# Two PSUM banks instead of four for the large products beside stick-breaking attention

## The chip, the cores and the metric

The kernel runs on one core of one Trainium2 chip. The metric is device time in microseconds (us), the median of several runs. In the text PE is TensorE's matmul pipe, DVE is VectorE, ACT is ScalarE, POOL is GpSimd and SP is SyncE, which here only issues DMAs. PSUM, where TensorE writes its results, has eight banks of 128x512 fp32 values; a tile here takes a whole bank.

## What is computed

A trunk of two layers on 512 tokens of width 1024. The first layer mixes tokens with a gated short convolution, the second with stick-breaking attention; both also attend to 256 memory tokens, and both end in a SwiGLU block. The change touches the second layer only, in these lines of the reference:

```python
kv = (rmsnorm(x, kv_norm) @ w_kv_shared).reshape(b, s_len, 2, SB_HEADS, HEAD_DIM)   # 12 heads of 64
k_sh, v_sh = kv[:, :, 0], kv[:, :, 1]
...
z = jnp.einsum("bhtd,bhsd->bhts", qb, kb) * scale          # 4 blocks of 128 queries
log_not = jnp.where(causal, jax.nn.log_sigmoid(-z), 0.0)
tail = lax.cumsum(log_not, axis=3, reverse=True) - log_not
a = jnp.where(causal, jnp.exp(jax.nn.log_sigmoid(z) + tail), 0.0)
outs.append(jnp.einsum("bhts,bhsd->bhtd", a, vb))
...
x = x + jnp.concatenate([y_main, y_mem], axis=-1) @ w_o[i]
x = x + swiglu(rmsnorm(x, ffn_norm[i]), w_gate[i], w_up[i], w_down[i])
```

## The kernel before

Every fp32 operand is split in two parts (`wh`, `wl` and the like: high part by an ACT copy, low part by a DVE subtraction), and each product is made of three matmuls: high x high, high x low, low x high (`three`, L345). So TensorE does three passes over all weights, and weights are split on the fly: they arrive by DMA in two `raw` buffers and are split into nine `w` buffers (L35, L36, L169), which are taken in turn and come free when the last matmul that reads them is done.

PSUM is shared by two groups of four banks. `acc` (L129) serves the large products: queries `q`, values `v`, keys `k`, the output projection `o` and its late part `ol`. `att` (L132) serves everything of attention: scores `z`, transposes `at`, the weighted sums `av`, and the gate and up products of the SwiGLU block. A tile takes its group's next bank in turn, and its first matmul waits until the tile that held the bank before has been read for the last time.

The order of work around the change is one program, in which the large products are the main work and stick-breaking is a generator (`stick`, L904) whose steps are slipped in between. After each few matmuls of the main work `lanes.pump` runs the steps that are due by a count of matmul columns (`STICK_PACE`). There are 48 steps: six pairs of heads, two heads in each, four blocks of queries. A step issues the scores `z` of its block (two matmuls), two sigmoids on ACT (`sn`, `sp`), two causal masks on POOL, a reversed running product on DVE (the scan of `sn`) and a multiplication (`sp`). Two steps later the weights are transposed on PE (`at`) and split (`aTh` on ACT, `aTl` on DVE). Five steps later, for every second block, the weighted sum `av` is taken (`weighted`, L939). When a head is done its sum is copied and added (`pv_s` on ACT, `ysf` on DVE), and when a pair is done the result is split into `ys` (ACT, then DVE).

The main work beside it is, in order: for three blocks of 256 columns, the values (`values`, L883: `by_token`, four token tiles) and the keys (two tiles); then the output projection `out_proj_late` (L665), for two halves of the columns, with the memory heads (`ym`) and the first four pairs `ys0` to `ys3` as its left side; then the last two pairs (`ol`), the norms, and the SwiGLU block (its first products are `gu`). `by_token` (L396) takes four banks, one a token tile. It runs a piece of the weights over all four tiles, then the next piece, so every bank is in use until the last piece. When the output projection asks for `ys` of a pair that is not yet issued, `ys_late` (L996) issues stick-breaking steps until it is (`lanes.until`).

After this a scheduler orders the instructions of each engine; on each engine they then run strictly in that order.

Of the kernel before, what the change touches and what calls it, by code (L numbers as in the profile page):

```python
# [9 lines left out]
F32 = mybir.dt.float32  # L10
# [6 lines left out]
P = 128  # L17
# [89 lines left out]
def trunk(ctx: ExitStack, tc: tile.TileContext, x, mem, mix_norm, a_in, conv_w, b_in,  # L107
# [13 lines left out]
    ps = ctx.enter_context(tc.tile_pool(name="ps", bufs=4, space=bass.MemoryType.PSUM))  # L121

    def slot(shape, dtype, name):
        return apool.tile(shape, dtype, tag="a", name=name)

    def t2(shape, dtype, name):
        return tpool.tile(shape, dtype, tag="t2", name=name)

    def acc(name):  # L129
        return ps.tile([P, 512], F32, tag="acc", name=name, bufs=4)  # L130

    def att(name):  # L132
        return ps.tile([P, 512], F32, tag="att", name=name, bufs=4)
# [211 lines left out]
    def three(dst, a, b, first, last):  # L345

        mm(dst, a(HI), b(HI), first, False)
        mm(dst, a(HI), b(LO), False, False)
        mm(dst, a(LO), b(HI), False, last)
# [46 lines left out]
    def by_token(w, pieces, c0, n, lhs, ntok, name, done, tail=1):  # L396


        banks = [acc(f"{name}{t}") for t in range(ntok)]
        got = []  # L400
        nk = sum(len(p) for p in pieces)
        at = 0
        for i, (kts, wp) in enumerate(rows(w, pieces, c0, n)):
            got.append((at, kts, wp))
            at += len(kts)
            if i >= len(pieces) - tail and i != len(pieces) - 1:
                continue
            for t in range(ntok):
                for a, ks, (wh, wl) in got:
                    for j, k in enumerate(ks):  # L410
                        three(banks[t][:, :n], lambda hl: lhs(k, hl, t), lambda hl: (wh, wl)[hl][:, j, :],
                              a + j == 0, a + j == nk - 1)
                        lanes.pump()
                if i == len(pieces) - 1:
                    done(t, banks[t])
            got = []
# [39 lines left out]
    banks = first.run(hmix, nx.chains, as_they_come)  # L456
# [6 lines left out]
    def queries(b, name):  # L463


        q = slot([P, 2, S], F32R, name)
        for hh in range(2):
            r = hh * HD
            own, other = slice(r, r + HD), slice(HD - r, P - r)
            nc.scalar.activation(q[own, hh, :], b[own, :], AF.Copy, scale=SCALE)  # L470
            nc.vector.scalar_tensor_tensor(q[other, hh, :], b[own, :], SCALE, q[own, hh, :].bitcast(F32),
                                           ALU.mult, ALU.subtract)
        return q
# [128 lines left out]
    for cc in range(3):  # L602
        cg, cus = [], []
        for c in range(2):
            f = 2 * cc + c
# [7 lines left out]
            t = t2([P, S], F32, f"cgs{f}")  # L613
            nc.scalar.activation(t, b, AF.Copy)
            cg.append(t)
        for c, get in enumerate(cols(a_in[0], 2 * MAIN + cc * 256)):
            f = 2 * cc + c
# [10 lines left out]
        for c, get in enumerate(cols(a_in[0], cc * 256)):  # L628
            f = 2 * cc + c
# [13 lines left out]
    def residual(t, hf, b, ss, name):  # L643
        part = xt[t][:, hf * 512:(hf + 1) * 512]
        nc.vector.tensor_tensor(part, b, part, ALU.add)
        if ss is not None:
            square_sum(ss[t], xt[t], hf, f"{name}{t}")
# [4 lines left out]
    def ylhs(ys):  # L652
        return lambda k, hl, t: ys(k)[:, hl, t * P:(t + 1) * P]
# [11 lines left out]
    def out_proj_late(layer, ys, last, opening, then):  # L665

        for hf in range(2):
            by_token(w_o[layer], [[6, 7], [0, 1], [2, 3]], hf * 512, 512, ylhs(ys), NT,
                     f"o{layer}{hf}", lambda t, b: residual(t, hf, b, None, f"oa{layer}"))
        wp = [list(rows(w_o[layer], [[4, 5]], hf * 512, 512))[0][1] for hf in range(2)]  # L670
        last()
        opening.prepare()
        ss = sums(f"sso{layer}")
        for t in range(NT):
            for hf in range(2):
                b = acc(f"ol{layer}{t}{hf}")
                for j, k in enumerate((4, 5)):
                    three(b, lambda hl: ylhs(ys)(k, hl, t), lambda hl: wp[hf][hl][:, j, :], j == 0, j == 1)
                    lanes.pump()
                residual(t, hf, b, ss, f"ob{layer}")  # L680
            then(t, rstd_of(ss[t], f"o{layer}{t}"))
# [222 lines left out]
    def stick(pace):  # L904
        weight, aT, pvs, yfs = {}, {}, {}, {}

        def weigh(p, hh, i):

            q, (kd, kl) = qs[p], ks[p]
            n, nm = (i + 1) * P, f"{p}{hh}{i}"  # L910
            z = att(f"z{nm}")[:, :n]
            scores_of(z, q, hh, i, kd[:, hh, :n], kl[:, hh, :n])
            sn = t2([P, S], F32, f"sn{nm}")
            sp = t2([P, S], F32, f"sp{nm}")
            nc.scalar.activation(sn[:, :n], z, AF.Sigmoid, scale=-1.0)
            causal(sn[:, i * P:n], 1.0)
            nc.scalar.activation(sp[:, :n], z, AF.Sigmoid)
            causal(sp[:, i * P:n], 0.0)
            back = sn[:, 1:n][:, ::-1]
            nc.vector.tensor_tensor_scan(back, back, back, 1.0, ALU.mult, ALU.bypass)  # L920
            nc.vector.tensor_tensor(sp[:, :n - 1], sp[:, :n - 1], sn[:, 1:n], ALU.mult)
            weight[p, hh, i] = sp
            if (p, hh, i) == (PAIRS - 1, 1, NT - 1):
                load_table(AF.Silu, sp[:, n - 1:n])

        def turn(p, hh, i):
            n, u, nm = (i + 1) * P, i % 2, f"{p}{hh}{i}"
            if u == 0:
                aT[p, hh, i // 2] = [slot([P, 4, 256], F32R, f"aT{hl}{nm}") for hl in "hl"]
            sp = weight.pop((p, hh, i))  # L930
            b = att(f"at{nm}")
            for j in range(i + 1):
                transpose(b[:, j * P:(j + 1) * P], sp[:, j * P:(j + 1) * P], ident)
            src = b[:, :n].rearrange("p (j c) -> p j c", j=i + 1)
            dst = [a[:, 0:i + 1, u * P:(u + 1) * P] for a in aT[p, hh, i // 2]]
            hi_of(dst[HI], src)
            lo_of(dst[LO], src, dst[HI])

        def weighted(p, hh, ip):  # L939
            head, r = 2 * p + hh, hh * HD  # L940
            if ip == 0:
                pvs[head] = att(f"av{head}")
                if hh == 0:
                    yfs[p] = t2([P, S], F32, f"ysf{p}")
            pv, a = pvs[head], aT.pop((p, hh, ip))
            top = 2 * ip + 1
            for part, j in [(HI, 0)] + [(LO, j) for j in range(top + 1)] + [(HI, j) for j in range(1, top + 1)]:
                s0 = P if j == top else 0
                mm(pv[0:P if part == HI else HD, ip * 256 + s0:(ip + 1) * 256], value(j, head, part == HI),
                   a[part][:, j, s0:256], part == HI and j == 0, part == HI and j == top)  # L950
            if ip == 1:
                stacked_pv(pvs.pop(head), r, yfs[p], f"s{head}")
                if hh == 1:
                    ymain[p] = split_y(yfs.pop(p), f"ys{p}")

        steps = [(p, hh, i) for p in range(PAIRS) for hh in range(2) for i in range(NT)]
        N = len(steps)
        for n in range(N + SUM_AFTER):
            if n < N:
                while ks[steps[n][0]] is None:  # L960
                    yield 1000
                weigh(*steps[n])
            if 0 <= n - TURN_AFTER < N:
                turn(*steps[n - TURN_AFTER])
            if 0 <= n - SUM_AFTER < N and steps[n - SUM_AFTER][2] % 2:
                p, hh, i = steps[n - SUM_AFTER]
                weighted(p, hh, i // 2)
            yield int(pace * (steps[min(n, N - 1)][2] + 1) / 2.5)

    banks = first.run(hq, nq.chains)  # L970
# [5 lines left out]
    for c2 in range(1, 3):  # L976
        for c, get in enumerate(cols(b_in[0], c2 * 256)):
            b = acc(f"q{c2}{c}")
            by_feature(b, get(), hq, 0, S)
            qs[2 * c2 + c] = queries(b, f"q{2 * c2 + c}")  # L980
    for c2 in range(3):
        values(c2)
        if c2 == 0:
            lanes.finish(mat)
        for c, get in enumerate(cols(w_kv_shared, c2 * 256)):
            b = acc(f"k{c2}{c}")
            by_feature(b, get(), hkv, 0, S)
            p = 2 * c2 + c
            kd = slot([P, 2, S], F32R, f"kd{p}")
            kl = key_lo[p % len(key_lo)]  # L990
            keys(b, kd, kl)
            ks[p] = kd, kl
            if p == 1:
                sticks = lanes.spawn(stick(STICK_PACE))
# [56 lines left out]
```

## Time and profile before

| | |
|---|---|
| median of 3 runs | 1145.6 us (1145.08 to 1145.99) |
| the profiled execution | 1145.12 us |
| its span, first to last instruction | 1143.4 us |
| PE busy, share of the span | 1130.9 us, 99% |
| DVE busy | 699.5 us, 61% |
| ACT busy | 524.1 us, 46% |
| mean granted TensorE clock | 0.998 |

The profile lists for each engine how long it was busy, what ended its idle time, and when each instruction started. Matmuls are pipelined, so their listed durations overlap: how much time one costs is read from the distance between the starts of consecutive ones. The names are those of the tiles, with their numbers left out: `o` is any tile of the output projection.

### The profile page before, as it was taken

To read this page: it belongs to the slowest core of one execution; us is meant where nothing else is said; L and a number is where in the kernel's file an instruction comes from. 1 tells how busy PE (TensorE), PEld (TensorE's weight loads), DVE (VectorE), ACT (ScalarE), POOL (GpSimd) and SP (SyncE) were. 2 spreads that over 40 slices of the span, in tenths; PEclk is the share of its full clock that TensorE was granted. 3 is DMA by queue.
4 is the path that set the end of the run, shared out by engine and by line. 5 is a ranking of instruction groups with operands and counts; after the bars stand their busy time and mean duration, and the time that the engine had idled before them with its cause. 6 is when DMAs were issued, how large, how long until landed. Compare 5 with 4: busy or idle time off the path is not lost.

```text
span 1143.4 us, 14862 instructions
## 1 busy us (share of the span) xinstructions
PE 1130.9 (99%) x5844; PEld 963.2 (84%) x5844; DVE 699.5 (61%) x1044; ACT 524.1 (46%) x896; POOL 76.3 (7%) x155
## 2 busy tenths in 40 slices
PE   9999999999999999999999999999999999999997
PEld 9898888988888888888988988788888888888886
DVE  5767453553774468434678799986546844485335
ACT  7555423533432344233666677665434332353223
POOL 1100000000000001000100123321000000000000
PEclk9999999999999999999999999999999999999999
DMA  8332422247332742414222211122274244542311
GB/s 259 111 111 74 144 78 74 74 142 190 111 111 74 219 108 79 141 62 130 75 74 75 74 56 56 38 75 92 74 220 123 66 143 149 109 148 76 126 57 74
DMA packets 97456, 122.10 MB, mean 107 GB/s; under 512 B 2217, under 2 KB 73963, under 8 KB 97387
## 3 DMA queue, kind: packets, MB, share of 16 engines
q1 hardware_dynamic: 93040, 112.73, 30.1%
q0 software_dynamic: 4224, 8.39, 4.3%
q8 instruction: 46, 0.75, 0.3%
q14 instruction: 23, 0.19, 0.1%
q10 hardware_dynamic: 123, 0.03, 0.0%
HBM read 119.05 MB, written 2.10 MB: 106 GB/s over the span
## 4 chain that ended last, share of the span: by engine, by line
PE 92%; issue 3%; DVE 2%; ACT 1%; POOL 1%; DMA 1%; POOLq 0%; ACTq 0%; SPq 0%; DVEq 0%
PE u L136 22%; PE g L136 19%; PE A_d L136 6%; PE d L136 5%; PE o L136 5%; PE N_d L136 4%; PE S_d L136 4%; PE gu L136 4%; PE bg L136 3%; PE v L136 3%; PE k L136 2%; PE pa L136 2%; PE cg L136 2%; PE q L136 1%; PE pb L136 1%
## 5 line engine op out<-in xcount | busy, mean ns | idle before, releaser
L157 DVE TENSOR_TENSOR wl<-raw,wh 128x1024 fp32r<-128x1024 f32 x180 | 220.0, 1222 | 281.3 <-PE u L136 136.5
L154 ACT ACTIVATE wh<-raw 128x1024 fp32r<-128x1024 f32 x180 | 191.0, 1061 | 264.6 <-PE u L136 75.8
L819 ACT ACTIVATE sg<-g 128x512 f32<-128x512 f32 x40 | 23.9, 598 | 105.5 <-PE g L136 105.5
L136 PE MATMUL g<-hffn0h,wh 128*128 128x512 f32 x160 | 62.3, 389 | 0.0
L136 PE MATMUL g<-hffn0l,wh 128*128 128x512 f32 x160 | 62.3, 389 | 0.0
L136 PE MATMUL g<-hffn1h,wh 128*128 128x512 f32 x160 | 62.3, 389 | 0.0
L136 PE MATMUL g<-hffn1l,wh 128*128 128x512 f32 x160 | 62.3, 389 | 0.0
L136 PE MATMUL g<-hffn0h,wl 128*128 128x512 f32 x160 | 62.2, 389 | 0.0
L136 PE MATMUL u<-hffn0h,wh 128*128 128x512 f32 x160 | 62.2, 389 | 0.0
L136 PE MATMUL u<-hffn0l,wh 128*128 128x512 f32 x160 | 62.2, 389 | 0.0
L136 PE MATMUL u<-hffn0h,wl 128*128 128x512 f32 x160 | 62.2, 389 | 0.0
L136 PE MATMUL g<-hffn1h,wl 128*128 128x512 f32 x160 | 62.2, 389 | 0.0
L136 PE MATMUL u<-hffn1h,wh 128*128 128x512 f32 x160 | 62.2, 389 | 0.0
L136 PE MATMUL u<-hffn1l,wh 128*128 128x512 f32 x160 | 62.2, 389 | 0.0
L136 PE MATMUL u<-hffn1h,wl 128*128 128x512 f32 x160 | 62.2, 389 | 0.0
L136 PE MATMUL d<-wh,hid 128*128 128x512 f32 x192 | 59.7, 389 | 0.0
L154 ACT ACTIVATE wh<-b_d 128x1024 fp32r<-128x1024 f32 x32 | 33.7, 1060 | 34.2 <-PE u L136 15.3
L920 DVE TENSOR_TENSOR_SCAN sn<-sn 128x127 f32<-128x127 f32 (+3 forms) x48 | 40.3, 840 | 4.8 <-POOL sn L901 4.4
L136 PEld LDWEIGHTS d<-wh,hid 128*128 128x128 f32 x192 | 36.0, 188 | 7.5
L157 DVE TENSOR_TENSOR wl<-b_d,wh 128x1024 fp32r<-128x1024 f32 x32 | 38.9, 1221 | 4.1 <-PE N_d L136 2.3
L136 PE MATMUL d<-wl,hid 128*128 128x512 f32 x96 | 37.4, 389 | 0.0
L136 PEld LDWEIGHTS u<-hffn0l,wh 128*128 128x128 f32 x160 | 30.0, 188 | 6.3
(777 smaller groups left out, 2937.9 us busy)
## 6 DMA issues: line engine op xcount, KB each, us to landing
raw<-in_w_gate_dram SPq DMA_DIRECT2D x22, 1024.0 KB, 5.3
raw<-in_w_up_dram SPq DMA_DIRECT2D x22, 1024.0 KB, 5.4
raw<-in_w_down_dram SPq DMA_DIRECT2D x12, 1024.0 KB, 6.6
raw<-in_a_in_dram SPq DMA_DIRECT2D x8, 1024.0 KB, 5.5
b_d<-in_w_down_dram SPq DMA_DIRECT2D x8, 1024.0 KB, 7.5
raw<-in_w_o_dram SPq DMA_DIRECT2D x12, 512.0 KB, 3.6
raw<-in_w_kv_shared_dram SPq DMA_DIRECT2D x6, 1024.0 KB, 5.0
raw<-in_w_mem_kv_dram SPq DMA_DIRECT2D x4, 1024.0 KB, 5.2
```

Of the source, the lines that this page charges most:

```text
L136: nc.tensor.matmul(dst, a, b, start=start, stop=stop)
L154: keep(nc.scalar.activation(dst, src, AF.Copy))
L157: keep(nc.vector.tensor_tensor(dst, src, hi.bitcast(F32), ALU.subtract))
L819: nc.scalar.activation(sg, bg, AF.Silu)
L920: nc.vector.tensor_tensor_scan(back, back, back, 1.0, ALU.mult, ALU.bypass)
```

## The change

`acc` now takes its banks from two groups of two (`acc` and `mid`) in turn, which makes four as before, except while a flag `few` is set. The flag is set after the queries' products, before the first values, and cleared in `out_proj_late` before the late part. While it is set, `acc` has two banks, and the weighted sums `av` take the two banks of `mid`; the four banks of `att` are then left to `z` and `at`. `by_token` no longer takes its four banks at the start: while the flag is set it waits for all pieces of the weights and then runs all of them for one token tile after the other, and each tile takes its bank when its turn comes.

```diff
+    few, turns = [False], [0]
+
     def acc(name):
-        return ps.tile([P, 512], F32, tag="acc", name=name, bufs=4)
+        turns[0] += 1
+        return ps.tile([P, 512], F32, tag="acc", name=name, bufs=2) if few[0] or turns[0] % 2 else mid(name)
+
+    def mid(name):
+        return ps.tile([P, 512], F32, tag="mid", name=name, bufs=2)
...
     def by_token(w, pieces, c0, n, lhs, ntok, name, done, tail=1):
-        banks = [acc(f"{name}{t}") for t in range(ntok)]
+        if few[0]:
+            tail = len(pieces)
+        banks = [acc(f"{name}{t}") for t in range(ntok) if tail < len(pieces)]
...
             for t in range(ntok):
+                if t == len(banks):
+                    banks.append(acc(f"{name}{t}"))
...
         last()
+        few[0] = False
         opening.prepare()
...
             if ip == 0:
-                pvs[head] = att(f"av{head}")
+                pvs[head] = mid(f"av{head}")
...
+    few[0] = True
     for c2 in range(3):
         values(c2)
```

How it moves instructions is seen at three places. In the names, the first number of `z412`, `at410`, `sp403` is the pair, the second the head in the pair, the third the block; `o101` is layer 1, first half of the columns, token tile 1; what follows a `_` is a running number.

On PE, where the output projection first reads `ys3`, the rows before are:

```order
L136 MATMUL o101_6471<-wh197_6672,ys2_6432 128x512
L136 MATMUL o101_6471<-wl197_6673,ys2_6432 128x512
L136 MATMUL o101_6471<-wh197_6672,ys2_6432 128x512
L136 MATMUL z412_6741<-kd4_6322,q4_5066 128x384
L136 MATMUL z412_6741<-kl0_4548,q4_5066 128x384
L143 MATMUL at410_6756<-ident_77,sp410_6683 128x128
L136 MATMUL av8_6760<-aTh400_6623,v20_6077 128x256
L136 MATMUL av8_6760<-aTl400_6624,v20_6077 64x256
L136 MATMUL av8_6760<-aTl400_6624,v20_6077 64x128
L136 MATMUL o100_6470<-wh197_6672,ys3_6711 128x512
L136 MATMUL o100_6470<-wl197_6673,ys3_6711 128x512
L136 MATMUL av8_6760<-aTh400_6623,v20_6077 128x128
```

and with the change they are:

```order
L143 MATMUL o101_6724<-wl194_6474,ym10_5099 128x512
L150 MATMUL at410_6713<-ident_77,sp410_6644 128x128
L143 MATMUL o101_6724<-wh194_6473,ym10_5099 128x512
L143 MATMUL o101_6724<-wh194_6473,ym11_5284 128x512
L143 MATMUL o101_6724<-wl194_6474,ym11_5284 128x512
L143 MATMUL o101_6724<-wh194_6473,ym11_5284 128x512
L143 MATMUL z413_6731<-kd4_6322,q4_5066 128x512
L143 MATMUL z413_6731<-kl0_4548,q4_5066 128x512
L143 MATMUL o100_6487<-wh197_6483,ys3_6672 128x512
L143 MATMUL o100_6487<-wl197_6484,ys3_6672 128x512
L150 MATMUL at411_6744<-ident_77,sp411_6682 128x128 x2
L143 MATMUL o101_6724<-wh195_6477,ys0_5848 128x512
```

Before, 54 matmuls of `o` stand ahead of the first that reads `ys3`: all that the first two pieces of the weights give to four token tiles, and a few of the third. Now 21 do: 15 of token tile 0, which are all that it has without `ys3`, and 6 of tile 1.

On PE, at the transposes of the last step, the rows before are:

```order
L136 MATMUL o113_6805<-wh202_7061,ys2_6432 128x512
L136 MATMUL o113_6805<-wl202_7062,ys2_6432 128x512
L136 MATMUL o113_6805<-wh202_7061,ys2_6432 128x512
L143 MATMUL at513_7108<-ident_77,sp513_7040 128x128 x4
L136 MATMUL o113_6805<-wh202_7061,ys3_6711 128x512
L136 MATMUL o113_6805<-wl202_7062,ys3_6711 128x512
L136 MATMUL o113_6805<-wh202_7061,ys3_6711 128x512
L136 MATMUL av11_7131<-aTh510_7015,v20_6077 128x256
```

and with the change they are:

```order
L143 MATMUL o111_7052<-wh200_6983,ys0_5848 128x512
L143 MATMUL o111_7052<-wl200_6984,ys0_5848 128x512
L143 MATMUL o111_7052<-wh200_6983,ys0_5848 128x512
L150 MATMUL at513_7062<-ident_77,sp513_7001 128x128 x4
L143 MATMUL o111_7052<-wh200_6983,ys1_6162 128x512
L143 MATMUL o111_7052<-wl200_6984,ys1_6162 128x512
L143 MATMUL o111_7052<-wh200_6983,ys1_6162 128x512
L143 MATMUL o111_7052<-wh202_6989,ys2_6432 128x512
```

Before, three matmuls of `o` were left when the last transposes came. Now 45 are left: nine of tile 1 of the second half, all 18 of tile 2 and all 18 of tile 3.

On DVE, where the order calls the scan of `sn` `SCALAR_TENSOR_TENSOR`, the second half's first weight pieces (`wl200`, `wl202`) are split at other places. Before, the rows around the first of them are:

```order
L157 TENSOR_TENSOR aTl310_6501<-at311_6531,aTh310_6500 128x2x128
L921 TENSOR_TENSOR sp313_6522<-sp313_6522,sn313_6521 128x511
L157 TENSOR_TENSOR wl200_6932<-raw198_6806,wh200_6931 128x1024
L920 SCALAR_TENSOR_TENSOR sn400_6558<-sn400_6558 128x127
L921 TENSOR_TENSOR sp400_6559<-sp400_6559,sn400_6558 128x127
L157 TENSOR_TENSOR aTl312_6569<-at312_6570,aTh312_6568 128x3x128
```

and with the change:

```order
L933 TENSOR_TENSOR sp503_6858<-sp503_6858,sn503_6857 128x511
L656 TENSOR_TENSOR x2_75<-o102_6814,x2_75 128x512
L164 TENSOR_TENSOR wl200_6984<-raw198_6976,wh200_6983 128x1024
L932 SCALAR_TENSOR_TENSOR sn510_6889<-sn510_6889 128x127
L933 TENSOR_TENSOR sp510_6890<-sp510_6890,sn510_6889 128x127
L164 TENSOR_TENSOR aTl502_6900<-at502_6901,aTh502_6899 128x3x128
```

It stood ahead of step 400, and now it stands ahead of step 510, behind the residual sum of tile 2; `wl202` moved likewise from ahead of step 410 to behind the scan of step 511.

## Rows read from the trace of the kernel before

**Rows 1.** The page: busy times, and the granted clock in 40 slices.

```profile
PE 1130.9 (99%) x5844; PEld 963.2 (84%) x5844; DVE 699.5 (61%) x1044; ACT 524.1 (46%) x896; POOL 76.3 (7%) x155
...
PEclk9999999999999999999999999999999999999999
```

**Rows 2.** Stretches: length, busy us of each engine, granted clock, DMA.

```profile
640.00:660.00 20.00, 20.00 (x152) 19.01 (x152) 18.17 (x31) 14.70 (x36) 6.07 (x17) 1.00 0.23 74
...
712.00:736.00 24.00, 22.75 (x124) 17.71 (x121) 21.84 (x38) 17.17 (x39) 9.39 (x20) 1.00 0.13 44
736.00:767.00 31.00, 30.11 (x163) 25.20 (x164) 28.61 (x48) 18.08 (x40) 9.83 (x20) 1.00 0.23 69
```

**Rows 3.** Waits of PE, 640 to 784 us: total, times, longest.

```profile
PE z L136 <- DVE aTl L157: 1.1, 2, 0.7
PE o L136 <- DVE kl L157: 0.6, 1, 0.6
PE ol L136 <- ACT ys L154: 0.4, 1, 0.4
```

**Rows 4.** PE in order of time: start, us, instruction, [idle before <- releaser].

```profile
735.92 0.50 PE L136 MATMUL o<-wh,ys 128*128 128x512 f32 x1
...
765.97 0.39 PE L136 MATMUL o<-wl,ys 128*128 128x512 f32 x1
766.19 0.63 PE L136 MATMUL o<-wh,ys 128*128 128x512 f32 x2
766.66 0.39 PE L136 MATMUL o<-wl,ys 128*128 128x512 f32 x1
...
783.72 0.39 PE L136 MATMUL gu<-hffn1h,wh 128*128 128x256 f32 x1
```

**Rows 5.** DVE in order of time, around the split of `ys3`.

```profile
721.40 0.68 DVE L921 TENSOR_TENSOR sp<-sp,sn 128x511 f32<-128x511 f32 x1
722.00 1.22 DVE L157 TENSOR_TENSOR wl<-raw,wh 128x1024 fp32r<-128x1024 f32 x1
723.40 0.48 DVE L920 TENSOR_TENSOR_SCAN sn<-sn 128x127 f32<-128x127 f32 x1 [0.19 <-POOL sn L901]
...
729.68 1.22 DVE L920 TENSOR_TENSOR_SCAN sn<-sn 128x511 f32<-128x511 f32 x1 [0.96 <-POOL sn L901]
...
733.13 0.48 DVE L920 TENSOR_TENSOR_SCAN sn<-sn 128x127 f32<-128x127 f32 x1 [0.19 <-POOL sn L901]
...
736.42 0.73 DVE L157 TENSOR_TENSOR ys<-ysf,ys 128x512 fp32r<-128x512 f32 x1
737.07 0.50 DVE L921 TENSOR_TENSOR sp<-sp,sn 128x255 f32<-128x255 f32 x1
```

**Rows 6.** PE in order of time, at values and the first keys.

```profile
621.72 0.28 PE L136 MATMUL v<-wh,hkvh 128*128 128x256 f32 x1
621.84 0.28 PE L136 MATMUL v<-wl,hkvh 128*128 128x256 f32 x1
...
643.50 0.28 PE L136 MATMUL v<-wh,hkvh 128*128 128x256 f32 x1
...
674.08 0.28 PE L136 MATMUL v<-wh,hkvh 128*128 128x256 f32 x1
...
681.61 0.36 PE L136 MATMUL v<-wh,hkvh 128*128 128x256 f32 x1
```

**Rows 7.** DVE in order of time, at the reads of values and keys.

```profile
621.53 0.68 DVE L521 TENSOR_TENSOR ymf<-pv,pv 64x512 f32<-64x512 f32 x1 [1.08 <-ACT pv L520]
...
624.24 0.41 DVE L157 TENSOR_TENSOR v<-v,v 128x256 fp32r<-128x256 f32 x1
...
643.77 0.69 DVE L157 TENSOR_TENSOR kl<-k,kd 64x512 fp32r<-64x512 f32 x1 [1.08 <-ACT kd L154]
...
680.70 0.69 DVE L157 TENSOR_TENSOR kl<-k,kd 64x512 fp32r<-64x512 f32 x1 [0.34 <-ACT kd L154]
```

**Rows 8.** The page: DMA issues, KB each, median us from issue to landing.

```profile
raw<-in_w_o_dram SPq DMA_DIRECT2D x12, 512.0 KB, 3.6
```

## The prediction, made before the changed kernel ran

> **What bounds the kernel now.** I read the page first: PE is busy for 99% of the span, and its clock is granted in full in all 40 slices [rows 1]. Nearly every microsecond in which PE waits is then a microsecond of the result, and little is to be won: PE's total work does not change, and the change can only add or take away waits. The stretches come next [rows 2]. In the span as a whole DVE is 61% busy, but while stick-breaking runs it is a second bound: 18.2 of 20 us from 640 to 660 and 50.5 of 55 us from 712 to 767. An order of work that needs DVE's results sooner than before finds no spare DVE time. Third, PE's waits in the affected stretch [rows 3]: 1.1 us of `z` for the DVE read that frees an `att` bank (twice), 0.6 us of `o` for the read of a key tile, 0.4 us of `ol` for `ys`. That is the change's target: four banks for `z` and `at` can take away at most about 1.1 us. Last, the order of time on PE and DVE [rows 4 to 7], for what two banks and the new order cost.
>
> **Step 1: the weighted sums leave the `att` banks.** This removes at most the 1.1 us [rows 3]. One of the two waits stands just ahead of the `ys3` stretch below, where DVE sets the pace anyway. I take 0.5 us off.
>
> **Step 2: two banks for values, keys and the output projection.** No instruction is added, but a tile must now be read before the next but one may begin. A value tile has 24 matmuls at 0.12 us (the distance of the starts in [rows 6]), so its neighbour covers 2.9 us of reading, plus the stick-breaking work that lies between; a key tile covers 24 x 0.23 = 5.5 us. The main work is in the same place against the steps until the projection begins, so the old times can be used, tile by tile:
> - Third value tile of the first block. PE comes to it where before it stood at 621.8 us [rows 6]. The first tile's DVE read stands in the new order behind the `ymf` that starts at 621.53 and takes 0.68, and takes 0.41 itself [rows 7]: the bank is free at 622.6. Wait 0.8 us.
> - First key tile: its bank is freed behind the last pair of memory heads; by the same count about 0.3 us.
> - Second value tile of the second block: PE stands there at about 643.6 [rows 6]; the second read of the key tile that holds the bank runs from 643.77 to 644.46 [rows 7]. Wait 0.85 us. Its successor, and the key tile after that, wait about 0.3 us each by the same count.
> - Second value tile of the third block: PE comes to it behind transposes, at 681.6 [rows 6]; the key tile that holds its bank is read to the end at 681.4 [rows 7]. No wait.
>
> The sum is 2.5 us. PE issues the scores too, so the steps move with it, and DVE has no room to make it up. The trace has no kernel with two banks, so the ends are: nothing, if the reads come a little sooner in the new order, and 4 us more, if the last case goes the other way (by main work alone that tile would come 36 x 0.12 = 4.3 us after the keys' end at 674.08 [rows 6], 3 us ahead of the read). I take 2.5. The Trainium skill (Perfetto Trace Analysis, section on optimizing tensor performance, matmuls) has independent matmul groups rotate through PSUM banks so that reading one overlaps the next group's matmuls. It speaks against this step, and by it the sum has the 2.5 us or more; by the wait of `o` behind a key tile, 0.6 us with four banks [rows 3], a wait of that kind is short, and the sum could do with less.
>
> **Step 3: token tile by token tile.** This is the largest term. Token tile 0 of the projection can do 15 matmuls before it needs `ys3`; before, 54 matmuls of four tiles stood ahead, now 21 do. PE reaches `ys3` with 33 matmuls of 0.23 us fewer behind it (three starts in 0.69 us [rows 4]), 7.6 us, less about half a microsecond of steps that come earlier: 7.0 us of work are put off. They come back after the stick-breaking: 45 matmuls of `o` are left at the last transposes instead of three. If `ys3` came 7 us sooner, this would be free. Does it? Its DVE split ended at 737.15, right when PE wanted it: PE began on `ys3` at 735.92 [rows 4, 5]. From the multiplication of step 313, which starts at 721.40, to that split DVE worked nearly without a gap. The new order takes out of this stretch two weight splits of 1.22 us and puts in one multiplication of 0.50: 1.9 us less. The scores no longer wait behind main work, so the idle 0.96 and twice 0.19 us [rows 5] can go, 1.3 us, and about half a microsecond of small gaps. So `ys3` comes some 3.7 us sooner, not 7. PE must wait for it, in several pieces, at the transposes of steps 401 to 411 and at `ys3`: +7.0 - 3.7 = +3.3 us.
>
> Behind `ys3` I leave the other waits at what they were: 47.8 us from the first use to the gate's first matmul [rows 4], of which the starts account for about 44.5. The 0.4 us of `ol` for `ys` may go, since ten matmuls of `ol` now stand between; but the moved splits can wait in turn. `wl200` needs a `w` buffer that token tile 3's first six matmuls free, and behind it in DVE's strict order stand the scans; a DVE wait there is a PE wait one step later. The loads of the late pieces start only when those splits free their `raw` buffers; they land 3.6 us after issue [rows 8] and are covered by about 2 us for the first, by nothing for the second, but behind the second PE has 45 matmuls in hand, 10 us. I put both at nothing. Ends of the step: -1 us (the 4.6 us that DVE is idle from 712 to 767 [rows 2] recovered, and the wait at the end gone) and +7 us (`ys3` no sooner).
>
> **Sum.** -0.5 + 2.5 + 3.3 = +5.3 us. Against the profiled execution's 1145.1 us (span 1143.4) that is 1150.4; the median of the runs before is 0.5 us higher than that execution, which I leave out: 1150.4 us. Less than 0.2% (2.3 us) either way cannot be told from no change.
>
> **Rivals.**
> - *The waits change place and nothing more.* The reads come early enough for two banks, since DVE and ACT have nothing else to wait for while PE stands, and the put-off matmuls hide the end of stick-breaking, where before `ol` waited for `ys` [rows 3]. Steps 2 and 3 then cost about 0.5 and 1: 1146.1 us, no change. Against it: the bank of the first case is freed by a chain from a memory head (idle 1.08 us for ACT [rows 7]), which no bank shortens.
> - *Faster: the steps run ahead.* If free `att` banks let the scores come so early that DVE never idles, it gains its idle time, 1.8 us in 640 to 660 and 2.2 us in 712 to 736 [rows 2], some 5 us or more up to `ys3`, and the 1.9 us of moved work. Then `ys3` comes 7 us sooner, steps 2 and 3 are free, and the waits of PE in the stretch go, 2.1 us [rows 3]: 1143.0 us. It decides this way if `ys3` is split before 730. Against it: only two scores ever waited for a bank, and most of the scans begin as soon as POOL is done, that is, they wait for a chain, not for a bank.
> - *Twice as bad: DVE blocked in its order.* Each of `wl200` and `wl202` waits 1 to 2 us for PE's matmuls on token tile 3 while PE waits for a scan behind it, and the third block's keys cost 4 us. +5.3 + 3 + 4: about 1157 us. For it: DVE takes nothing out of turn, so such a wait holds up every step behind it. Against it: in the order, the matmuls that free the buffers stand ahead of the transposes that need the scans.
> - *The clock.* While PE waits for `ys3` in pieces, its instructions there fill about two thirds of 7 us. The trace shows 1.00 in every stretch with matmuls, waits of up to 0.7 us included [rows 1, 3]. If the clock fell to its lower level of 1.2 GHz after such a stretch, the matmuls of the following few microseconds would take double: 3 us more, 1153 us. The Trainium skill (TensorE: Matmul & The Clock Gate, part on the psum-queue depth-cycling failure mode) tells of a kernel whose short idle times between matmul groups made the clock go back and forth; nothing in this trace shows it.
>
> **How the numbers follow.** The forecast has 0.53, no change 0.21, faster 0.12, blocked 0.1, the clock 0.04. The forecast's own range is 1148 to 1153.5; with the rival of no change on one side and part of the worse ones on the other I give 1144.5 to 1155. Faster by over 0.2%: 0.11, the rival without its upper end. Within 0.2%: 0.21 and a small part of the forecast and of the faster rival, 0.23. Slower: 0.66.
>
> **What would show it.** Step 1: no `z` waits for `aTl`. Step 2: `v` waits for the reads `v` and `kl` around 622 and 645, and the first scores come about 1 us later. Step 3: `at` and `o` of PE wait for `sp` and `ys` between the projection's start and the split of `ys3`, some 3 us more than before; DVE has no wait there; that split ends some 12 us after the multiplication of step 313 begins, not 15.75; and from the first use of `ys3` to the gate's first matmul it takes about 55 us instead of 47.8. A split of `ys3` before 730, or a PE without waits there, would show the prediction wrong; so would a DVE that idles for `o` at the moved splits, in the other direction.

## The result, and the profile after

The changed kernel takes 1153.2 us (median; 1152.98 to 1153.96) against 1145.45 (1145.08 to 1145.99) for the kernel before, run beside it: the ratio is 1.0071, 95% interval [1.0059, 1.0082]. It is slower, as forecast, and 2.8 us beyond the forecast of 1150.4. The profiled execution has a span of 1151.3 us against 1143.4.

The page of the changed kernel, busy times and the granted clock, answers to [rows 1]:

```profile
PE 1131.0 (98%) x5844; PEld 962.8 (84%) x5844; DVE 699.3 (61%) x1044; ACT 523.5 (45%) x896; POOL 77.0 (7%) x155
...
PEclk9999999999999999999999999999999999999999
```

PE has the same work (1130.9 before) at the same clock, so the 7.9 us by which the span grew are waits. PE's waits from 640 to 784 us (total, times, longest), against [rows 3]:

```profile
PE at L150 <- DVE sp L933: 2.6, 5, 0.9
PE at L150 <- DVE aTl L164: 2.3, 4, 0.9
PE at L150 <- ACT sp L929: 1.4, 1, 1.4
PE v L143 <- DVE kl L164: 1.1, 2, 0.7
PE ol L143 <- DVE x L656: 0.7, 1, 0.7
PE av L143 <- DVE aTl L164: 0.3, 1, 0.3
PE at L150 <- ACT sn L927: 0.2, 1, 0.2
```

The waits of `z` for `aTl` are gone, 1.1 us, and 8.6 us of others are there, where 1.0 stood. Two more, 1.5 us, stand ahead of 640, at a value tile (0.69, row 622.67 below) and at the first key tile (0.79). The stretches of the changed kernel (length, busy us of PE, PEld, DVE, ACT and POOL, granted clock, DMA), against [rows 2]:

```profile
640.00:660.00 20.00, 19.20 (x143) 17.92 (x142) 16.18 (x26) 13.25 (x31) 5.10 (x14) 1.00 0.16 54
...
712.00:736.00 24.00, 19.62 (x119) 15.87 (x118) 23.29 (x42) 18.96 (x46) 10.83 (x23) 1.00 0.04 14
736.00:767.00 31.00, 30.20 (x166) 24.93 (x165) 28.61 (x48) 18.76 (x41) 10.31 (x20) 1.00 0.16 49
```

From 712 to 736 the two engines have changed places: before, PE was busy for 22.75 us and DVE for 21.84; now PE is busy for 19.62 and DVE for 23.29 of 24. (These are the same times in both profiles; the changed kernel is by then 4.6 us behind in its work.) The clock stayed at 1.00 all the same.

PE of the changed kernel in order of time (start, us, instruction, idle before it and what ended it), at the values, in the third block, in the burst of steps before `ys3`, and at the gate:

```profile
622.67 0.36 PE L143 MATMUL v<-wh,hkvh 128*128 128x256 f32 x1 [0.69 <-DVE v L164]
...
646.57 0.36 PE L143 MATMUL v<-wh,hkvh 128*128 128x256 f32 x1 [0.71 <-DVE kl L164]
...
683.65 0.66 PE L150 MATMUL at<-ident,sp 128*128 128x128 f32 x4 [0.93 <-DVE aTl L164]
684.71 0.39 PE L143 MATMUL v<-wh,hkvh 128*128 128x256 f32 x1 [0.40 <-DVE kl L164]
...
716.60 0.48 PE L143 MATMUL o<-wh,ym 128*128 128x512 f32 x1
...
726.85 0.63 PE L150 MATMUL at<-ident,sp 128*128 128x128 f32 x4 [1.41 <-ACT sp L929]
...
736.69 0.50 PE L143 MATMUL o<-wh,ys 128*128 128x512 f32 x1
...
791.59 0.39 PE L143 MATMUL gu<-hffn1h,wh 128*128 128x256 f32 x1 [0.28 <-DVE hffn1l L330]
```

Three places say where the time went. All of PE's work ahead of the projection is the same in both kernels, and its first matmul, 711.98 before, starts at 716.60: 4.6 us lost by then. The first use of `ys3`, 735.92 before [rows 4], starts at 736.69. The gate's first matmul, 783.72 before [rows 4], starts at 791.59: 7.9 us lost. From the projection to `ys3` PE is 3.85 us quicker than before with 33 matmuls fewer in front, and from `ys3` to the gate it takes 54.9 us instead of 47.8. By blocks, from PE's rows: the first block of values and keys takes 2.0 us more than before, the second 0.9, the third 1.8, and the way from the projection to the gate 3.3.

DVE of the changed kernel in order of time, against [rows 5] and [rows 7]:

```profile
621.52 0.68 DVE L532 TENSOR_TENSOR ymf<-pv,pv 64x512 f32<-64x512 f32 x1 [1.08 <-ACT pv L531]
622.12 0.73 DVE L164 TENSOR_TENSOR v<-v,v 128x256 fp32r<-128x256 f32 x2
...
683.19 0.41 DVE L164 TENSOR_TENSOR aTl<-at,aTh 128x256 fp32r<-128x256 f32 x1
...
725.96 0.74 DVE L933 TENSOR_TENSOR sp<-sp,sn 128x511 f32<-128x511 f32 x1
...
730.10 0.94 DVE L932 TENSOR_TENSOR_SCAN sn<-sn 128x383 f32<-128x383 f32 x1
730.96 0.26 DVE L164 TENSOR_TENSOR aTl<-at,aTh 128x128 fp32r<-128x128 f32 x1
731.14 0.67 DVE L933 TENSOR_TENSOR sp<-sp,sn 128x383 f32<-128x383 f32 x1
...
737.19 0.69 DVE L164 TENSOR_TENSOR ys<-ysf,ys 128x512 fp32r<-128x512 f32 x1
```

The multiplication of step 313 begins at 725.96 and the split of `ys3` ends at 737.88: 11.9 us without one wait, where it was 15.75 before.

### The profile page after: what moved, and what is told of

Same layout as the page of the kernel before. It is cut to its first block, busy times and chain, and to the rows that moved or that the text cites. A ratio compares the mean times of both kernels' runs of the same rounds, so it can differ in the third digit from the quotient of the medians.

```text
span 1151.3 us, 14843 instructions
## 1 busy us (share of the span) xinstructions
PE 1131.0 (98%) x5844; PEld 962.8 (84%) x5844; DVE 699.3 (61%) x1044; ACT 523.5 (45%) x896; POOL 77.0 (7%) x155
## 4 chain that ended last, share of the span: by engine, by line
PE 88%; DVE 4%; ACT 3%; issue 2%; DMA 1%; POOL 1%; POOLq 0%; DVEq 0%; ACTq 0%; SPq 0%
PE u L143 22%; PE g L143 19%; PE A_d L143 6%; PE o L143 5%; PE d L143 5%; PE N_d L143 4%; PE S_d L143 4%; PE gu L143 4%; PE bg L143 3%; PE k L143 3%; PE pa L143 2%; PE cg L143 2%; PE v L143 2%; PE pb L143 1%; PE q L143 1%
## 5 line engine op out<-in xcount | busy, mean ns | idle before, releaser
L143 PEld LDWEIGHTS u<-hffn1h,wl 128*128 128x128 f32 x160 | 30.1, 188 | 6.3
```

The source lines that it names most:

```text
L143: nc.tensor.matmul(dst, a, b, start=start, stop=stop)
```

## The experiments

The times of all runs, each beside the kernel before on the same chip. The kernel before took 1145.2 to 1145.5 us each time. The last two columns are read from PE's rows of the profiled execution: how much later than before the projection and the gate begin, counted from the first value matmul (614.12 us before; projection 711.98, gate 783.72).

| kernel | time, us | ratio to before | projection | gate |
|---|---|---|---|---|
| the changed kernel | 1153.22 | 1.0071 [1.0059, 1.0082] | +4.6 | +7.9 |
| order alone, four banks | 1149.89 | 1.0041 [1.0026, 1.0056] | +1.3 | +4.8 |
| values alone | 1150.49 | 1.0049 [1.0034, 1.0064] | +4.6 | +5.0 |
| values alone, four banks | 1146.54 | 1.0012 [1.0002, 1.0021] | +1.3 | +1.0 |
| projection alone | 1148.47 | 1.0026 [1.0016, 1.0037] | 0.0 | +3.3 |
| projection in pairs | 1156.70 | 1.0099 [1.0084, 1.0114] | +4.6 | +11.3 |
| before, multiplications on POOL | 1145.65 | 1.0002 [0.9993, 1.0012] | +1.8 | +0.4 |
| changed, multiplications on POOL | 1154.19 | 1.0079 [1.0064, 1.0094] | +5.0 | +8.7 |
| changed, sums in `att` | 1153.99 | 1.0075 [1.0060, 1.0090] | +5.3 | +8.3 |
| changed, steps earlier | 1155.78 | 1.0089 [1.0075, 1.0102] | +9.4 | +10.1 |
| before, steps earlier | 1148.06 | 1.0020 [1.0011, 1.0029] | +4.5 | +2.2 |
| projection alone, steps earlier | 1150.20 | 1.0040 [1.0027, 1.0052] | +4.6 | +5.1 |
| changed, less DVE work | 1153.55 | 1.0071 [1.0057, 1.0085] | +4.7 | +8.4 |

(With the steps earlier, more of their work stands ahead of the projection; there the first of the two columns is not a loss.)

The count starts at that matmul because the profiles are apart by up to 0.6 us already there, where every kernel has had the same work. The kernel before, and the one with the values alone and four banks:

```profile
614.12 0.28 PE L136 MATMUL v<-wh,hkvh 128*128 128x256 f32 x1
...
614.74 0.28 PE L143 MATMUL v<-wh,hkvh 128*128 128x256 f32 x1
```

### The order without the banks

Order alone, four banks; the same edit, and the flag cleared after the keys, gives "values alone, four banks":

```diff
-        return ps.tile([P, 512], F32, tag="acc", name=name, bufs=2) if few[0] or turns[0] % 2 else mid(name)
+        return ps.tile([P, 512], F32, tag="acc", name=name, bufs=4)
...
-                pvs[head] = mid(f"av{head}")
+                pvs[head] = att(f"av{head}")
```

> Token tile by token tile in values and projection as in the changed kernel, but acc keeps its four banks and av stays in att. If the projection's cost comes from its order (33 matmuls put off, ys3 bound by DVE) it stays without the two banks: about +3 us over the kernel before for the projection and +0.5 for the values, 1149 us. If the two banks are the whole cost, it is the kernel before: 1145.5 us.

It came out at 1149.9: of the 7.8 us, 4.6 are the order's and some 3 the banks'. PE has no wait of `v` or `k` for a read left, and its projection starts 1.3 us late instead of 4.6.

### Values alone, and projection alone

```diff
-                pvs[head] = mid(f"av{head}")
+                pvs[head] = (mid if few[0] else att)(f"av{head}")
...
+    few[0] = False      # values alone: behind the last keys, ahead of ys_late
-    few[0] = True       # projection alone: not ahead of the values,
+    few[0] = True       #   but behind the last keys, ahead of ys_late
```

> Values and keys as in the changed kernel (two banks, token tile by token tile, av in its own two), the projection as before with four banks. My theory: PE is 4.6 us late when the projection begins, as in the changed kernel, and DVE has no room to make it up: 1150 us. Rival: DVE is the bound of the whole stretch and PE had slack, so that the lateness is absorbed behind: 1146 us.

> Values and keys as before, the projection as in the changed kernel (two banks, token tile by token tile, av in its own two). My theory: +7.0 us of put-off work, -3.7 us for ys3 sooner, +3.3 us: 1148.7 us. Rival: the projection's order is only late because the values made it late, and costs nothing alone: 1145.5 us.

Values alone came out at 1150.5 (5.2 us more than before; its four runs lie between 1149.97 and 1152.54), projection alone at 1148.5 (3.2 more). Together 8.5, against 7.8 for the whole: within the scatter of the first, the two parts make up the whole. In the kernel with the values alone the 4.6 us by which the projection is late are still there at the gate (5.0): nothing behind it makes them up. PE's waits of that kernel, 600 to 800 us:

```profile
PE at L150 <- DVE aTl L164: 1.9, 3, 0.9
PE o L143 <- DVE kl L164: 1.3, 1, 1.3
PE v L143 <- DVE kl L164: 1.1, 2, 0.7
PE k L143 <- DVE v L164: 0.8, 1, 0.8
PE v L143 <- DVE v L164: 0.7, 1, 0.7
```

and of the kernel with the projection alone, in the same stretch:

```profile
PE at L150 <- DVE sp L933: 3.6, 5, 1.4
PE ol L143 <- DVE x L656: 0.7, 1, 0.7
```

The first list is waits for a PSUM bank to be read throughout. Of the second, the 3.6 us are the chain of the steps; `ol` waits for the residual sum that reads an `o` tile, and does so for 0.7 us with four banks too.

### The values' order with four banks

> Only the values go token tile by token tile; four banks, av in att and the projection as before. If the values' cost is the wait for two banks: +0.5 us at most, 1146 us. If it is the order (both weight pieces needed at once, reads at other places in DVE's order): 1149 us or more, like the run with two banks.

It came out at 1146.5: 1.3 us for the order of the values, and the remaining 3.95 of the 5.25 us for their two banks. (The weighted sums are in `att` here and in `mid` in the kernel with the values alone. The next run finds that move worth nothing or a little gain, so it does not explain the 3.95.) The Trainium skill (Perfetto Trace Analysis, section on optimizing tensor performance, matmuls) wants independent matmul groups to rotate through PSUM banks, so that the reading of one overlaps the next. The trace agrees: the waits of `v` and `k` for reads, 2.6 us with two banks, are gone with four. The 3.95 us are what two banks instead of four cost here. With the same method the projection's order costs 3.35 us with four banks (1149.89 less 1146.54) and 3.2 with two: there the number of banks makes no difference that shows.

### The weighted sums back in `att`

```diff
-                pvs[head] = mid(f"av{head}")
+                pvs[head] = att(f"av{head}")
```

> As the changed kernel with two banks for the large products, but the weighted sums stay in att and mid is not used while stick-breaking runs. If banks of their own for the sums are worth what the waits of z for aTl were, it is 0.5 to 1 us slower than the changed kernel: 1154 us. If they are worth nothing (the changed kernel's at waits for aTl instead), it is the same: 1153.2 us.

It came out at 1154.0; 0.8 us more than the changed kernel by the medians, but the intervals of the two ratios overlap: own banks for the sums are worth half a microsecond or so, possibly nothing. PE's waits, 600 to 800 us:

```profile
PE z L143 <- DVE aTl L164: 1.6, 4, 0.6
...
PE at L150 <- DVE aTl L164: 0.4, 1, 0.4
```

Here `z` waits 1.6 us for `aTl` and `at` 0.4; in the changed kernel `z` never does, and `at` does for 2.3. So the sums' own banks did not remove the wait for DVE's subtraction, they moved it from `z` to `at`. With only `z` and `at` in the group, the two take its four banks by turns, and the row at 683.65 fits this: the four transposes start right behind the subtraction of an earlier `at` (683.19 and 0.41 us).

### Token tiles two by two

```diff
+        for t0 in range(0, ntok, 2):
+            banks = {t: acc(f"{name}{t}") for t in (t0, t0 + 1)}
+            at = 0
+            for i in range(len(pieces)):
...
+                for t in (t0, t0 + 1):
```

> As the changed kernel, but the projection takes token tiles two by two in its two banks, piece by piece, so that 30 instead of 21 of its matmuls stand ahead of the first that reads ys3 (54 in the kernel before). If what is put off behind ys3 is the projection's cost, 9 matmuls less of it are worth 2 us: 1151.2 us. If the cost is the two banks' reuse in the projection, no change: 1153.2 us.

It came out at 1156.7, 3.5 us worse than one by one, and nearly all of that is the clock. Stretches of 4 us, columns as above:

```profile
716.00:720.00 4.00, 3.90 (x26) 3.17 (x24) 3.65 (x7) 3.00 (x9) 1.89 (x4) 1.00 0.00 0
720.00:724.00 4.00, 2.28 (x9) 1.67 (x8) 4.00 (x9) 3.93 (x9) 1.61 (x3) 0.78 0.00 0
724.00:728.00 4.00, 4.00 (x17) 3.26 (x16) 3.66 (x7) 1.45 (x5) 0.98 (x3) 0.79 0.00 0
```

and PE in order of time in the same kernel:

```profile
721.98 0.41 PE L150 MATMUL at<-ident,sp 128*128 128x128 f32 x2 [1.72 <-DVE sp L957]
722.15 0.66 PE L143 MATMUL o<-wh,ys 128*128 128x512 f32 x1
722.61 0.63 PE L143 MATMUL o<-wl,ys 128*128 128x512 f32 x1
```

Behind a wait of 1.72 us the clock is granted at its lower level, and a matmul of `o` takes 0.43 us where it took 0.23. The two windows lack 0.22 and 0.21 of 4 us, 1.7 us of work. It fell a second time from 736 to 740, to 0.58 in that window, another 1.7 us: by this estimate 3.4 of the 3.5 us. Without the two falls the kernel would be at the changed kernel's time, not 2 us below it: the nine matmuls that now stand ahead of `ys3` again brought nothing that shows, so this run gives the count of put-off matmuls no support. The prediction had priced such a fall at 3 us, and in the changed kernel it does not come.

### The multiplications on POOL

One edit, in the kernel before and in the changed one:

```diff
-            nc.vector.tensor_tensor(sp[:, :n - 1], sp[:, :n - 1], sn[:, 1:n], ALU.mult)
+            nc.gpsimd.tensor_tensor(sp[:, :n - 1], sp[:, :n - 1], sn[:, 1:n], ALU.mult)
```

> The kernel before with the multiplication behind each scan (sp) on POOL instead of DVE: 2.0 us a head off DVE. Control for the next run. PE bounds the kernel before, its order is the same, and its waits in the stretch come to 2.6 us: 1143 to 1146 us if POOL is quick enough; slower, 1148 us or more, if the longer chain of a step through POOL shows up at the transposes.

> The changed kernel with the same multiplication on POOL. If DVE's work sets when ys3 is ready, some 3 us of multiplications leave DVE between the end of step 313 and the split of ys3, that split comes about 3 us sooner, and the cost against its control falls from 7.8 to about 5 us: 1150 us. If it is the chain of a step (score, sigmoid, mask, scan, transposition), whose length grows with POOL, ys3 comes no sooner: 1153 us or more.

In the kernel before the time does not change: the projection begins 1.8 us late and the gate 0.4, so most of the delay is made up between them. That PE has `o` matmuls in hand there fits this, and is not shown. In the changed kernel it was to win 3 us and lost one. The clock is part of that: it was granted at 0.88 and 0.69 in the windows from 732 to 740, 1.7 us of work, so that without the fall the gain would be some 0.7 us by this estimate. PE's longest group of waits is now

```profile
PE at L150 <- POOL sp L933: 6.9, 7, 1.6
```

and DVE is busy for 19.79 of the 24 us from 712 to 736, where it was for 23.29. A multiplication takes 0.86 us (median) on POOL and 0.53 on DVE, and it stands in the chain from a score to its transposes. The run shows PE waiting for this chain once it is longer; it doesn't tell whether DVE's work bounds the burst otherwise.

### The steps one key tile earlier

```diff
-            if p == 1:
+            if p == 0:
                 lanes.spawn(stick(STICK_PACE))
```

> The kernel before, with its 48 stick-breaking steps spawned one key tile earlier (behind the first key tile of the first block instead of the second; the first pairs' keys are there by then). Theory (in this kernel ys3 and its successors are late because DVE sets the pace from the first step on): DVE gets about 5.5 us of time at 630 to 640 that it did not use, so the steps run up to 5 us ahead at ys3, PE's 2 to 4 us of waits in 640 to 784 shrink, and the time is about 1144 us, some 1.4 us less than before. Rival (PE has its work in hand at ys3 in the order of before, so earlier steps are worth nothing): 1145.5 us.

> The changed kernel, with the steps spawned one key tile earlier. Theory (step 3 of the prediction: the 7 us of put-off matmuls would be free if ys3 were split 7 us sooner, it was only 3.9): the steps come up to 5 us sooner, of which the values' two banks leave a part; PE's waits in the burst before ys3 fall by some 3 us, the first use of ys3 comes some 3 us sooner against the start of the projection, and the time is 1150 us against 1153.2. From the first use of ys3 to the gate it stays near 55 us. Rival (ys3 is late by the chain of each step, or by the banks, not by its start): 1153 us, and the first use of ys3 as late as in the changed kernel.

> The projection alone token by token with two banks (values and keys as before), with the steps spawned one key tile earlier. Theory: without the early steps it took 1148.5 us, 3.1 more than before; if ys3 comes up to 5 us sooner, most of this goes: 1145.8 us, and the first use of ys3 comes about 3 us sooner than in that kernel. Rival (two banks and the order cost what they cost whatever DVE has done): 1148.5 us.

All three came out slower, by 2.6, 2.6 and 1.7 us than the same kernel with the steps where they were. The steps do run ahead (in the changed kernel with earlier steps the first use of `ys3` comes 16.8 us after the projection's start instead of 20.1), but three longer waits take the place of the shorter ones. PE of the kernel before with earlier steps:

```profile
640.28 0.30 PE L143 MATMUL at<-ident,sp 128*128 128x128 f32 x1 [0.98 <-POOL sp L901]
...
686.63 0.39 PE L136 MATMUL v<-wh,hkvh 128*128 128x256 f32 x1 [1.37 <-DVE kl L157]
...
721.53 0.66 PE L143 MATMUL at<-ident,sp 128*128 128x128 f32 x4 [1.94 <-ACT sp L917]
721.95 0.61 PE L136 MATMUL o<-wh,ym 128*128 128x512 f32 x1
722.36 0.63 PE L136 MATMUL o<-wl,ym 128*128 128x512 f32 x1
```

ACT of that kernel, just ahead of the longest:

```profile
719.81 1.20 ACT L154 ACTIVATE kd<-k 64x512 fp32r<-64x512 f32 x2 [0.90 <-DVE kl L157]
721.04 0.28 ACT L915 ACTIVATE sn<-z 128x128 f32<-128x128 f32 x1
721.21 0.27 ACT L917 ACTIVATE sp<-z 128x128 f32<-128x128 f32 x1
```

The transposes start when the sigmoid that reads a newer `z` ends (721.48), which fits a wait for its bank; ACT takes that sigmoid in turn, behind the copies of a key tile that had waited 0.90 us for DVE. Then the clock falls, `o` takes 0.41 us, and the stretches show it:

```profile
720.00:724.00 4.00, 2.47 (x10) 2.13 (x11) 2.70 (x6) 3.57 (x9) 1.09 (x4) 0.77 0.00 0
724.00:728.00 4.00, 4.00 (x20) 3.31 (x19) 3.09 (x6) 1.72 (x5) 0.85 (x4) 0.81 0.02 4
```

What they lack of full speed is 0.23 and 0.19 of 4 us, 1.7 us of work. With the wait itself this one place costs more than the 2.6 us by which the kernel is slower, so the steps' lead may have been worth a little elsewhere; that was not isolated. The clock fell in the other two as well: with the projection alone to 0.79 in both windows from 720 to 728, 1.7 us of work, as much as that kernel lost; in the changed kernel to 0.75 and 0.83 from 688 to 696 and to 0.94 and 0.63 from 724 to 732, 3.4 us by the same estimate, more than its 2.6. So these runs do not settle whether DVE's time at 630 to 640 us, which the theory wanted to use, is worth anything.

### Less work for DVE

```diff
+        def once(p, hh):
+            return 2 * p + hh in (7, 8)
...
-            lo_of(dst[LO], src, dst[HI])
+            if not once(p, hh):
+                lo_of(dst[LO], src, dst[HI])
...
-                   a[part][:, j, s0:256], part == HI and j == 0, part == HI and j == top)
+                   a[0 if once(p, hh) else part][:, j, s0:256], part == HI and j == 0, part == HI and j == top)
```

> The changed kernel, with the low part of the transposed weights of heads 7 and 8 left out (the high part's tile is read in its place, so PE has the same matmuls and the output of these two heads is not the reference's). This takes eight subtractions off DVE, 3.8 us, six of them (0.53, 0.68, 0.26, 0.39, 0.53, 0.67 us, 3.1 us in all) between the multiplication of step 313 and the split of ys3, and nothing off the chain from a score to its transposes. Theory (DVE alone sets when ys3 is split, as step 3 says): the split comes some 3 us sooner against that multiplication, 8.9 us instead of 11.9, PE's waits in the burst shrink by as much, the first use of ys3 is near 733.7 us, and the time near 1150. Rival (each step's chain through PE, ACT, POOL and DVE sets it, as in the kernel whose multiplications are on POOL): DVE gets idle time in its place, ys3 comes less than 1 us sooner, and the time stays above 1152.

The time did not move, 1153.55, and the split of `ys3` ends 10.6 us behind the multiplication of step 313: 1.3 us sooner, not 3. DVE of this kernel in order of time:

```profile
726.01 0.75 DVE L933 TENSOR_TENSOR sp<-sp,sn 128x511 f32<-128x511 f32 x1
...
729.51 0.94 DVE L932 TENSOR_TENSOR_SCAN sn<-sn 128x383 f32<-128x383 f32 x1
730.55 0.64 DVE L933 TENSOR_TENSOR sp<-sp,sn 128x383 f32<-128x383 f32 x1
...
735.82 0.78 DVE L164 TENSOR_TENSOR ys<-ysf,ys 128x512 fp32r<-128x512 f32 x1
```

Neither theory had this. DVE still waits for no other engine between these rows, so the rival's idle time did not come. But the subtractions had cost less than their length. A multiplication reads the scan in front of it and starts 0.10 us behind its end (729.51 + 0.94 = 730.45, then 730.55), while the subtraction, which reads something else, starts before its predecessor's listed end (730.10 + 0.94 = 731.04, and `aTl` at 730.96). So the scan at 730.10 with a subtraction behind it and the scan at 729.51 without one both have their multiplication 1.04 us after their start: that subtraction of 0.26 us cost nothing. Of 3.1 us, 1.3 were to be had.

And these 1.3 us were spent again: the first use of `ys3` came 1.3 us sooner than in the changed kernel, with four matmuls of `o` and the two scores of step 413, some 1.4 us, no longer in front of it. PE's waits in the burst did not shrink: 4.1 us in the changed kernel and 4.7 here (720 to 740 us). So DVE's rows show it without a pause up to `ys3`; that PE would finish sooner if DVE did less is not shown.

## Why the prediction was right in direction and 2.8 us off

**Step 1, -0.5: half right.** No `z` waits for `aTl`, as said. A gain of 0.5 fits the run with the sums back in `att` (0.8 by the medians, possibly nothing). What the prediction missed is the other side: the wait for `aTl` went over to `at`, 2.3 us of it.

**Step 2, +2.5: the mechanism held, the size failed.** With step 1 it was to be +2.0; it was 4.6 at the projection's start, and 5.25 us in the time of the kernel with the values alone. Tile by tile:
- First block: 0.8 forecast for the third value tile, 0.69 in the profile (622.67); the first key tile waited 0.8 instead of 0.3. The keys began 1.9 us late, the first scores 2.0 (forecast about 1).
- Second block: 0.85 forecast for the second value tile, 0.71 in the profile. The third block's first value tile was 2.8 us late, against a count of 2.5 for the whole step. Up to here the count was nearly right.
- Third block: "No wait". This is the step that failed. The projection began 1.8 us later still. PE waited 0.40 us for `kl` at the tile the prediction had named, and 1.9 us in three waits of `at` for `aTl` between 674 and 702, where before only 0.3 us stood. The prediction had looked at the tile's own bank only, not at the transposes just ahead of it, which wait for a DVE that has a read of the keys in front (`kl` at 682.01, then the subtraction at 683.19). With the sums back in `att` the waits between 674 and 702 are 1.2 us of `at` for `sp` and 0.4 of `z` for `aTl`, and the projection begins no sooner: which tile waits goes by the banks, and the delay stays. And most of the 1.8 us, about 1.3, also comes with four banks, by the values' order alone: counted from its first value matmul, that kernel is on time at the third block's first tile (674.69, less the 0.61 us of its later start, against 674.08) and 1.3 us late at the projection. The prediction had a term for the banks of the values and none for their order. What makes the order cost this is not isolated; PE's waits between 674 and 702 us are 0.9 us in that kernel, for `sp` and `ysf`, against 0.3.

**Step 3, +3.3: right in size and in its signs.** Projection alone cost 3.2 us. From the projection to `ys3` the forecast was 3.7 us sooner, and it was 3.85; from `ys3` to the gate 7.0 us more, and it was 7.1 (54.9 us against "about 55"). The split of `ys3` ended 11.9 us after the multiplication of step 313, against "some 12". PE's waits between 702 and 740 rose from 1.2 to 4.1 us, against "some 3 us more". DVE waited 0.2 us in the burst. The moved weight splits cost nothing that shows.

**The reason given for step 3's size, DVE, is only partly tested.** That DVE has no pause left is in the profile; what PE gains from less DVE work was not to be shown with two runs that tried, because one lengthened the chain and had a fall of the clock, and the other let the order of PE move. The pairs, with fewer matmuls put off, gained nothing that shows either.

**The rivals.** No change and faster are excluded by the interval. DVE was not blocked at the moved splits. The clock stayed at 1.00 in the changed kernel, so that rival's 1153 us agrees with the measured time by chance; behind longer waits it did fall, in other runs.

## What to carry to other kernels

Before a bank is taken from a stream of products, count for every reuse not only when the bank's reader ends but what stands ahead of that reader in its engine's queue, and do so for the neighbours on the matmul engine too: where the reading engine has no spare time, the wait turns up at the next tile that needs it. Work that can fill a wait is worth most in front of it: the matmuls moved behind `ys3` came back at the end here, 7.1 us of them, and `ys3` came only 3.85 us sooner. An engine without a pause in a stretch says that it works there, not that each instruction less on it saves its listed length. And where an experiment makes a wait longer, look at the granted clock before reading its time: in five runs here a fall of it, 1.7 us each, hid what the edit itself was worth.

## What the runs showed that was not expected

- *The clock and the length of a wait.* Between 600 and 800 us PE's longest wait was 1.41 us in the changed kernel, 1.40 with the projection alone and 1.32 with the values alone, and the granted clock was 1.00 in every 4 us window there. Waits of 1.72 us (pairs), 1.94 (before, steps earlier), 1.92 (projection alone, steps earlier), 1.94 and 1.79 (changed, steps earlier) were each followed by windows with the clock at 0.63 to 0.94, and 1.57 with another of 1.31 close behind (changed, multiplications on POOL) by one at 0.69. One fall, in the kernel with pairs at 736 to 740, had no wait over 0.8 us just in front of it. The Trainium skill (TensorE: Matmul & The Clock Gate, part on the psum-queue depth-cycling failure mode) tells of short idle times between matmul groups that make the clock go back and forth; the many waits of the changed kernel had no fall behind them, and all falls but one stood behind longer waits, so the length of the last wait alone does not tell.
- *A dependent instruction on DVE.* In the changed kernel's rows a multiplication that reads the scan just in front of it starts about 0.1 us behind its end, and an independent instruction mostly 0.08 us before its predecessor's listed end; the subtraction of 0.26 us between the two was free.
- *Earlier is not sooner.* Starting the steps 4.5 us earlier (first score at 635.60 instead of 640.06) made the kernel before 2.6 us slower, with three waits and one fall of the clock that the later start did not have.
